# A two-layer attention encoder: part of the output product is enlarged in block A's stage, and its sum with x goes from VectorE to ScalarE and GpSimd

## Chip, cores, metric

The kernel runs on one core of one Trainium2 chip. The metric is the device time of one execution in microseconds (us), the median of three. TensorE (PE) multiplies, VectorE (DVE), ScalarE (ACT) and GpSimd (POOL) work element by element, and SyncE's queue (SP) issues the DMA transfers. A copy out of PSUM, the memory into which PE writes, is called an eviction.

## What is computed

The reference runs two layers over x (1024 rows by 1024 features). Cut to what matters:

```python
for l in range(2):
    h = rms_norm(x, norm_g[l]);  proj = h @ w_in[l]
    ya = dilated_attention(qa, ka, va, slopes) * silu(ag)   # block A: 4 heads
    yb = dense_attention(qb, kb, vb) * silu(bg)             # block B: 6 heads
    yc = dense_attention(qc, kc, vc) * silu(cg)             # block C: 6 heads
    y  = concatenate([ya, yb, yc])                          # 1024 features
    x  = x + y @ w_out[l]
```

Everything is fp32. Each product is done as three matmuls: both factors are split into a high part and a low part (hi and lo), and hi·hi, hi·lo and lo·hi are summed in PSUM.

## The kernel before

**Stages.** Each layer runs through the projections, six dense heads (block B), block A's stage, six dense heads (block C) and the out stage. In the profiled execution block A's stage lies at about 440 to 530 us in layer 0 and 1165 to 1255 us in layer 1.

**Order.** The heads and block A are written as small functions (`qk`, `soft`, `tv_t`, `a_s`, `a_t`, `f_mm` and so on) that `put(slot, f, priority)` enters in a table; slots are walked in order, and within a slot by priority. ACT executes in the order of this program. For PE, DVE, POOL and SP a scheduler decides the order ahead of time, and every engine then keeps to its own list: an instruction that waits holds up all that stand behind it on its engine.

**Block A's heads.** For each head `a_s` multiplies queries and keys into PSUM (L889 to L895), DVE adds a table and takes minima (L902, L905), ACT takes exponentials (L912, L914). A chain of small steps then finds the scales of three patterns: DVE L943, ACT L948, DVE L954, L955, L956, L958 and L961, PE L969 and DVE L975. GpSimd multiplies the probabilities by the scales, 8 times L984 (window patterns) and 8 times L988 (class pattern) for each head. PE transposes them (L1001, L1006, L1007), ACT and DVE split the result into hi and lo (L774, L775), and PE multiplies with the values (L1030 to L1044, first line for each form).

**The early part of the out product.** y is held as eight chunks of 128 features. Chunk k is split into `yh[k]` and `yl[k]` by `fin_split` (ACT L828, GpSimd L829) as soon as its two heads are done. Chunks 2 and 3 come from the first four heads of block B, chunk 4 from the last two. The output has eight blocks m of 128 features. For m = 2 to 7 the products with chunks 2 and 3 are done in block A's stage, in two halves of 512 columns: `f_load` fetches the weights and splits them on GpSimd (L1091, L1092) and fetches x; `f_mm` does six matmuls for a half into one PSUM bank (L1104, L1105, L1106); `f_add` adds that bank to x on DVE (L1110); a DMA stores the sum as `x_part`. One half follows the other after two slots, one m the other after five. The out stage does the rest (L1246 to L1248) and adds `x_part`.

**Buffers.** The T tag has four PSUM banks, shared by the transposes, the small products of the chain, the heads' sums (acc) and the halves of `f_mm`. The H tag has six SBUF buffers of 128x512.

Of the kernel before, what the change touches and what calls it, by code (L numbers as in the profile page):

```python
# [9 lines left out]
F32R = mybir.dt.float32r  # L10
I32 = mybir.dt.int32
AF = mybir.ActivationFunctionType
ALU = mybir.AluOpType
AX = mybir.AxisListType

P = 128
# [6 lines left out]
AH, BH, CH = 4, 6, 6  # L23
N_U = 28

EARLY_K, EARLY_M = (2, 3), range(2, 8)


@with_exitstack
def hybrid_encoder(  # L30
# [7 lines left out]
    nc = tc.nc  # L38
    V, G, A, T = nc.vector, nc.gpsimd, nc.scalar, nc.tensor
# [9 lines left out]
    def nm(s):  # L49
        uid[0] += 1  # L50
        return f"{s}_{uid[0]}"

    def U(dt=F32, shape=(P, SEQ)):
        return sp.tile(list(shape), dt, tag="U", name=nm("u"), bufs=N_U)

    def QB(dt=F32, shape=(P, 1152)):
        return sp.tile(list(shape), dt, tag="QB", name=nm("qb"), bufs=8)

    def H(dt=F32, shape=(P, 512)):
        return sp.tile(list(shape), dt, tag="H", name=nm("h"), bufs=6)  # L60

    def WR(dt=F32, shape=(P, 512)):
        return sp.tile(list(shape), dt, tag="Wr", name=nm("wr"), bufs=3)
# [13 lines left out]
    def PT():  # L77
        return pp.tile([P, 512], F32, tag="T", name=nm("T"), bufs=4)
# [4 lines left out]
    def f32(ap):  # L83
        return ap.bitcast(F32)
# [95 lines left out]
    ws = Stream()  # L180


    def x_prepare(k, x32, g_sb, xh, xl, parts=(slice(0, SEQ),)):
        hi, lo = U(F32R), U(F32R)
        for s in parts:
            A.activation(hi[:, s], x32[:, s], AF.Copy, scale=g_sb[:, k:k + 1])
            V.scalar_tensor_tensor(lo[:, s], x32[:, s], g_sb[:, k:k + 1], f32(hi[:, s]), ALU.mult, ALU.subtract)
        xh.append(hi)
        xl.append(lo)
# [28 lines left out]
    x_scr = dp.tile([SEQ, SEQ], F32, name="x_scr")  # L218
# [37 lines left out]
    MV = 2  # L256
# [10 lines left out]
    def layer(l, xh, xl, ss, g, bg_x):  # L267
# [7 lines left out]
        x_part = dp.tile([SEQ, SEQ], F32, name=nm("x_part"))  # L275
# [6 lines left out]
        for k in range(8):  # L282
            if bg_x is not None:
                bg_x(k)
            wh, wl = ws.next(3)
# [9 lines left out]
            for m, half in order:  # L295
                w = slice(m * P, m * P + P)
                o = bk[m][half]
                s = slice(half * 512, half * 512 + 512)
# [90 lines left out]
        for k in range(8):  # L389
            w = ws.next(3)  # L390
# [37 lines left out]
        for c in range(NCH):  # L428
            s = slice(c * P, (c + 1) * P)
            pq = PS()  # L430
            for half in range(2):
                o = pq[:, half * 512:half * 512 + 288]
                w = slice(half * 288, half * 288 + 288)
# [6 lines left out]
        for c in range(NCH):  # L440
            s = slice(c * P, (c + 1) * P)
# [641 lines left out]
        Fw, Fx, Fp = {}, {}, {}  # L1083

        def f_load(m):
            n = len(EARLY_K) * P
            raw = WR()[:, :n]
            both = H(F32R)
            hi, lo = both[:, :n], both[:, n:2 * n]
            nc.sync.dma_start(raw.rearrange("p (k c) -> p k c", c=P), w_out[l, m, :, EARLY_K[0]:EARLY_K[-1] + 1, :])  # L1090
            G.tensor_scalar(hi, raw, 1.0, 1.0, ALU.mult, ALU.mult)  # L1091
            G.tensor_tensor(lo, raw, f32(hi), ALU.subtract)  # L1092
            Fw[m] = (hi, lo)
            t = Fx[m] = U()
            nc.sync.dma_start(t, (x_t if l == 0 else x_scr)[m * P:(m + 1) * P, :])

        def f_mm(m, half):
            ps = Fp[m, half] = PT()
            hi, lo = Fw[m]
            s = slice(half * 512, half * 512 + 512)  # L1100
            n = len(EARLY_K)
            for i, k in enumerate(EARLY_K):
                w = slice(i * P, i * P + P)
                T.matmul(ps, hi[:, w], yh[k][:, s], start=(i == 0), stop=False)  # L1104
                T.matmul(ps, hi[:, w], yl[k][:, s], start=False, stop=False)  # L1105
                T.matmul(ps, lo[:, w], yh[k][:, s], start=False, stop=(i == n - 1))  # L1106

        def f_add(m, half):
            t = Fx[m][:, half * 512:half * 512 + 512]
            V.tensor_tensor(t, Fp.pop((m, half)), t, ALU.add)  # L1110
            if half:
                nc.sync.dma_start(x_part[m * P:(m + 1) * P, :], Fx.pop(m))


        base_a = 16 * BH
# [10 lines left out]
        def put(s, f, pri=5):  # L1126
            at_slot.setdefault(s, []).append((pri, len(at_slot.get(s, [])), f))


        for i, hd in enumerate(heads):  # L1130
            for c in range(NCH):
                s = start[hd] + 2 * c - LAG_D
# [4 lines left out]
        def a_slot(k):  # L1137
            return base_a + AS0 + AD * k // 2

        for h in range(AH):  # L1140
            for m in range(4):
                s = a_slot(4 * h + m)
# [3 lines left out]
            s = a_slot(4 * h + 3) + 1  # L1146
# [9 lines left out]
        for i, hd in enumerate(heads):  # L1156
            for half in range(2):
                for j in range(8):
                    s = start[hd] + 8 * half + j
                    put(s, lambda hd=hd, half=half, j=j: tv_t(hd, half, j), 1)  # L1160
                    put(s + DV, lambda hd=hd, half=half, j=j: tv_v(hd, half, j), 9)
                s = start[hd] + 8 * half + 8 + DV
# [6 lines left out]
        for h in range(AH):  # L1169
            for i in range(8):  # L1170
                s = base_a + AT0 + 8 * h + i
# [4 lines left out]
                    put(base_a + AT0 + 8 * h + FA[0] + half, lambda h=h, half=half: fin_gate(h // 2, half), 6)  # L1176
                    put(base_a + AT0 + 8 * h + FA[1] + half, lambda h=h, half=half: fin_split(h // 2, half), 6)
        F0, FN, FP, FL = -10, 5, 6.5, 8
        for m in EARLY_M:
            s = base_a + F0 + FN * (m - EARLY_M[0])  # L1180
            put(s - FL, lambda m=m: f_load(m), 9)
            for half in range(2):
                put(s + 2 * half, lambda m=m, half=half: f_mm(m, half), FP)
                put(s + 2 * half + 1, lambda m=m, half=half: f_add(m, half), 6)

        turns = (-23, -22, -19, -17)
        for i, hd in enumerate(heads):
            kind, h = hd
            s = start[hd]
# [10 lines left out]
        for h in range(AH):  # L1200
            s = a_slot(4 * h)
# [34 lines left out]
        nss = QB()[:, :SEQ] if l + 1 < DEPTH else None  # L1236
        ng = load_gains(l + 1) if l + 1 < DEPTH else None

        def out_part(ps, w2, ks, halves=(0, 1)):
            for k in ks:  # L1240
                wh, wl = w2[k // 4]
                w = slice((k % 4) * P, (k % 4) * P + P)
                for half in halves:
                    s = slice(half * 512, half * 512 + 512)
                    o = ps[half] if isinstance(ps, list) else ps[:, s]
                    T.matmul(o, wh[:, w], yh[k][:, s], start=(k == 0), stop=False)  # L1246
                    T.matmul(o, wh[:, w], yl[k][:, s], start=False, stop=False)  # L1247
                    T.matmul(o, wl[:, w], yh[k][:, s], start=False, stop=(k == 7))  # L1248

        def out_half(m, ps, half):  # L1250
            s = slice(half * 512, half * 512 + 512)
            xr = H()
            nc.sync.dma_start(xr, (x_part if m in EARLY_M else x_scr)[m * P:(m + 1) * P, s])
            V.tensor_tensor(xr, ps, xr, ALU.add)
            nc.sync.dma_start(out_t[m * P:(m + 1) * P, s], xr)

        def out_end(m, ps):
            xr = QB()[:, :SEQ]
            src = x_part if m in EARLY_M else x_t if l == 0 else x_scr
            nc.sync.dma_start(xr, src[m * P:(m + 1) * P, :])  # L1260
            V.tensor_tensor(xr, ps, xr, ALU.add)
            if l + 1 < DEPTH:
                nc.sync.dma_start(x_scr[m * P:(m + 1) * P, :], xr)
                x_prepare(m, xr, ng["x"], nxh, nxl)
                x_square(m, xr, nss)
            else:
                nc.sync.dma_start(out_t[m * P:(m + 1) * P, :], xr)
# [5 lines left out]
        first = {}  # L1273

        def out_first(m, k):
            if k == 0:
                first[m] = (PS(), [ws.next(), ws.next()])
            out_part(*first[m], [k])

        todo = [(m, k) for m in range(2) for k in range(7) if (m not in EARLY_M or k not in EARLY_K)]  # L1280
        for i, (m, k) in enumerate(todo):
            put(min(end, end - OF + i * ON // 2), lambda m=m, k=k: out_first(m, k), OP)
        slots(end + 1)
        for m in range(2):
            out_part(*first[m], [7])
            out_end(m, first[m][0])
        for m in range(2, 8):
            if m == 7 and l + 1 == DEPTH:
                w2 = [ws.next(), ws.next()]
                both = [PT(), PT()]  # L1290
                for half in range(2):
                    out_part(both, w2, [k for k in range(8) if m not in EARLY_M or k not in EARLY_K], (half,))
                    out_half(m, both[half], half)
                break
            ps = PS()
            out_part(ps, [ws.next(), ws.next()], [k for k in range(8) if m not in EARLY_M or k not in EARLY_K])
            out_end(m, ps)
        return nxh, nxl, nss, ng

# [1 line left out]
    for l in range(DEPTH):  # L1301
        for k in range(8):
            ws.add(w_lat[l, k * P:(k + 1) * P, :], (P, 384))
        for k in range(8):
            ws.add(w_v[l, k * P:(k + 1) * P, :], (P, 416))
        for k in range(8):
            ws.add(w_c[l, k * P:(k + 1) * P, :], (P, 512))
        for k in range(8):
            ws.add(w_a[l, k * P:(k + 1) * P, :], (P, 512))
        for m in range(8):  # L1310
            for kh in range(2):
                ws.add(w_g[l, m, :, 4 * kh:4 * kh + 4, :], (P, 4, P))
        ws.hold()
        for m in range(8):
            n = EARLY_K[0] if m in EARLY_M and EARLY_K[-1] == 3 else 4
            ws.add(w_out[l, m, :, 0:n, :], (P, n, P), True, V if m >= MV else None)
            ws.add(w_out[l, m, :, 4:8, :], (P, 4, P), True, V if m >= MV else None)


    warm = PT()  # L1320
# [126 lines left out]
```

## Time and profile before

| | |
|---|---|
| median of three | 1462.73 us (1462.49 to 1464.2) |
| profiled execution, its own time | 1465.32 us |
| its span, first to last instruction | 1463.4 us |
| mean granted TensorE clock | 0.999 |
| PE busy | 1445.4 us, 99% |
| DVE busy | 1094.0 us, 75% |
| ACT busy | 899.0 us, 61% |
| POOL busy | 570.8 us, 39% |

The profiled execution took 2.6 us more than the median, and 1.9 us of it lie outside the span. A share is an average over the whole span; the engines' loads in block A's stage differ from it and stand in a group of their own below. A matmul of 512 columns is listed with a duration of 0.39 us, but matmuls overlap, and what one costs PE is the distance from its start to the next one's.

### The profile page before, as it was taken

The numbers are of one execution on the slowest core, as the hardware profiler recorded it, in microseconds if no ns is written. First come the engines' busy times: TensorE is split into PE (matmuls) and PEld (weight loads), VectorE is DVE, ScalarE is ACT, GpSimd is POOL, SyncE is SP. The second block draws the span as 40 slices with busy tenths as digits, with TensorE's granted clock in tenths as the row PEclk, the third lists the DMA queues.
The fourth block names the chain that finished last, engine by engine and source line by source line (L and its number), as shares of the span: only waits on it lengthen the run. The fifth ranks groups of instructions, "written<-read, shape, count | busy, mean of one in ns | idle before, by whom it ended". The sixth has DMA issues, their size and how long they took to land.

```text
span 1463.4 us, 23131 instructions
## 1 busy us (share of the span) xinstructions
PE 1445.4 (99%) x7912; PEld 1228.4 (84%) x7912; DVE 1094.0 (75%) x1997; ACT 899.0 (61%) x1678; POOL 570.8 (39%) x516
## 2 busy tenths in 40 slices
PE   9999999999999999999999999999999999999999
PEld 7998888888888888888889988888888888888887
DVE  6749767488888889994726597574888788899932
ACT  6563234488888779893425723353888886899720
POOL 5304441135455465550322054211454555655400
PEclk9999999999999999999999999999999999999999
DMA  6272126710286831112522611465103688121142
GB/s 214 78 252 62 52 98 209 211 44 30 50 200 200 243 90 44 44 34 93 192 81 82 246 37 51 158 199 162 58 30 75 167 250 226 30 60 28 58 160 101
DMA packets 118134, 171.81 MB, mean 117 GB/s; under 512 B 11520, under 2 KB 72320, under 8 KB 118016
## 3 DMA queue, kind: packets, MB, share of 16 engines
q1 hardware_dynamic: 118016, 170.32, 38.2%
q8 instruction: 63, 1.03, 0.3%
q14 instruction: 55, 0.45, 0.1%
HBM read 109.47 MB, written 60.82 MB: 116 GB/s over the span
## 4 chain that ended last, share of the span: by engine, by line
PE 90%; DVE 5%; ACT 2%; DMA 1%; issue 1%; POOL 0%; SPq 0%; ACTq 0%; DVEq 0%; POOLq 0%
PE S L752 15%; PE T L781 11%; PE acc L794 6%; PE acc L793 6%; PE T L661 4%; PE T L659 4%; PE T L660 4%; PE S L1248 3%; PE S L1246 3%; PE S L1247 3%; PE S L215 2%; PE S L214 2%; PE S L213 2%; PE T L697 1%; PE T L215 1%
## 5 line engine op out<-in xcount | busy, mean ns | idle before, releaser
L775 DVE TENSOR_TENSOR wl<-T,wh 128x512 fp32r<-128x512 f32 x440 | 296.7, 685 | 69.9 <-ACT wh L774 67.7
L774 ACT ACTIVATE wh<-T 128x512 fp32r<-128x512 f32 x440 | 261.0, 596 | 112.7 <-PE T L781 78.1
L768 POOL TENSOR_SCALAR u<-u,rec 128x1024 f32<-128x1024 f32 x192 | 216.0, 1125 | 279.8 <-DVE rec L767 164.1
L752 PE MATMUL S<-u,u 96*128 96x512 f32 (+1 forms) x960 | 269.2, 410 | 0.4
L754 DVE TENSOR_REDUCE nmax<-S 128x1 f32<-128x1024 f32 x192 | 233.5, 1216 | 24.0 <-PE S L752 23.4
L781 PEld LDWEIGHTS T<-ident,u 128*128 128x128 f32 x1536 | 190.8, 140 | 49.0 <-DVE wl L775 0.4
L781 PE MATMUL T<-ident,u 128*128 128x128 f32 x1536 | 230.0, 272 | 0.0
L761 ACT ACTIVATE u<-S,nmax 128x1024 f32<-128x1024 f32 x192 | 213.2, 1110 | 0.3
L142 POOL TENSOR_TENSOR wl<-wr,wh 128x512 fp32r<-128x512 f32 (+2 forms) x48 | 75.1, 1567 | 321.6 <-ACT wh L138 310.7
L752 PEld LDWEIGHTS S<-u,u 96*128 96x128 f32 (+1 forms) x960 | 167.1, 189 | 27.8 <-ACT u L761 1.2
L138 ACT ACTIVATE wh<-wr 128x512 fp32r<-128x512 f32 (+2 forms) x96 | 56.9, 596 | 157.6 <-PE S L214 97.3
L659 PE MATMUL T<-u,wh 128*128 128x512 f32 x256 | 102.1, 399 | 0.0
L661 PE MATMUL T<-u,wl 128*128 128x512 f32 x256 | 100.1, 391 | 0.0
L660 PE MATMUL T<-u,wh 128*128 128x512 f32 x256 | 99.9, 390 | 0.0
L793 PE MATMUL acc<-wh,u 128*128 128x512 f32 x192 | 84.5, 440 | 0.0
L793 PE MATMUL acc<-wh,qb 128*128 128x512 f32 x192 | 82.8, 431 | 0.0
L794 PE MATMUL acc<-wl,u 128*128 128x512 f32 x192 | 76.1, 396 | 2.5 <-DVE wl L775 2.5
L1246 PE MATMUL S<-u,qb 128*128 128x512 f32 x196 | 78.0, 398 | 0.0
L1248 PE MATMUL S<-u,qb 128*128 128x512 f32 x196 | 77.1, 394 | 0.0
L1247 PE MATMUL S<-u,qb 128*128 128x512 f32 x196 | 76.8, 392 | 0.0
L794 PE MATMUL acc<-wl,qb 128*128 128x512 f32 x192 | 76.1, 396 | 0.1
L142 DVE TENSOR_TENSOR wl<-wr,wh 128x512 fp32r<-128x512 f32 (+2 forms) x48 | 41.3, 861 | 44.5 <-ACT wh L138 44.4
(294 smaller groups left out, 3330.3 us busy)
## 6 DMA issues: line engine op xcount, KB each, us to landing
u<-qk_c SPq DMA_DIRECT2D x40, 256.0 KB, 4.8
wr<-in_w_g_dram SPq DMA_DIRECT2D x32, 256.0 KB, 2.6
gates<-h SPq DMA_DIRECT2D x32, 256.0 KB, 2.5
qk_c<-u SPq DMA_DIRECT2D x16, 512.0 KB, 4.1
u<-gates SPq DMA_DIRECT2D x16, 512.0 KB, 4.5
qb<-qk_a SPq DMA_DIRECT2D x32, 256.0 KB, 6.0
vb<-u SPq DMA_DIRECT2D x16, 384.0 KB, 3.3
u<-vb SPq DMA_DIRECT2D x12, 512.0 KB, 4.6
```

The lines of the kernel that those rows point to most:

```text
L659: T.matmul(ps[half], wh[:, w], xh[k][:, s], start=(k == 0), stop=False)
L660: T.matmul(ps[half], wh[:, w], xl[k][:, s], start=False, stop=False)
L661: T.matmul(ps[half], wl[:, w], xh[k][:, s], start=False, stop=(k == 7))
L752: T.matmul(ps[:, w], q[:, s], k[:, w], start=(i == 0), stop=(i == len(terms) - 1))
L754: V.tensor_reduce(nmax, ps, op=ALU.max, axis=AX.X, negate=True)
L761: A.activation(p, ps, AF.Exp, bias=nmax, accum_out=den)
L768: G.tensor_scalar(p, p, rec, 1.0, ALU.mult, ALU.mult)
L774: A.activation(ph, ps, AF.Copy)
L775: V.tensor_tensor(pl, ps, f32(ph), ALU.subtract)
L781: T.transpose(ps[:, i * P:(i + 1) * P], Pt[hd, 4 * half + i][0][:, j * P:(j + 1) * P], ident)
L793: T.matmul(acc, w, ph, start=(j == 0), stop=False)
L794: T.matmul(acc, w, pl, start=False, stop=(j == 7))
```

## The change

A table `EARLY` says for each m which chunks are done early. For m = 2, 3 and 4 these stay 2 and 3; for m = 5, 6 and 7 chunk 4 comes in. A half of those m has nine matmuls in place of six, and the out stage three fewer. `f_load` then splits 128x384 in place of 128x256 and takes two H buffers, since hi and lo no longer fit in one. For all twelve halves of a layer `f_add` takes one more H buffer: ACT copies the PSUM bank into it, and GpSimd adds it to x. The rest (`late`, `out_part`) keeps the indices of the remaining weights in step.

```diff
-EARLY_K, EARLY_M = (2, 3), range(2, 8)
+EARLY = {2: (2, 3), 3: (2, 3), 4: (2, 3), 5: (2, 3, 4), 6: (2, 3, 4), 7: (2, 3, 4)}
+
+def late(m):
+    e = EARLY.get(m, ())
+    n = e[0] if e else 4
+    return tuple(range(n)), tuple(k for k in range(n, 8) if k not in e)
...
         def f_load(m):
-            n = len(EARLY_K) * P
+            ks = EARLY[m]
+            n = len(ks) * P
             raw = WR()[:, :n]
-            both = H(F32R)
-            hi, lo = both[:, :n], both[:, n:2 * n]
-            nc.sync.dma_start(raw.rearrange("p (k c) -> p k c", c=P), w_out[l, m, :, EARLY_K[0]:EARLY_K[-1] + 1, :])
+            if 2 * n <= 512:
+                both = H(F32R)
+                hi, lo = both[:, :n], both[:, n:2 * n]
+            else:
+                hi, lo = H(F32R)[:, :n], H(F32R)[:, :n]
+            nc.sync.dma_start(raw.rearrange("p (k c) -> p k c", c=P), w_out[l, m, :, ks[0]:ks[-1] + 1, :])
             G.tensor_scalar(hi, raw, 1.0, 1.0, ALU.mult, ALU.mult)
             G.tensor_tensor(lo, raw, f32(hi), ALU.subtract)
...
-            n = len(EARLY_K)
-            for i, k in enumerate(EARLY_K):
+            n = len(EARLY[m])
+            for i, k in enumerate(EARLY[m]):
                 w = slice(i * P, i * P + P)
...
         def f_add(m, half):
             t = Fx[m][:, half * 512:half * 512 + 512]
-            V.tensor_tensor(t, Fp.pop((m, half)), t, ALU.add)
+            c = H()
+            A.activation(c, Fp.pop((m, half)), AF.Copy)
+            G.tensor_tensor(t, c, t, ALU.add)
             if half:
                 nc.sync.dma_start(x_part[m * P:(m + 1) * P, :], Fx.pop(m))
```

What this does to the engines' lists is shown at three places of layer 0. Line numbers after the change are higher by 8 up to L1088 (L984 is L992 and L988 is L996); `f_mm` is L1116 to L1118, the copy L1123, the add L1124 and `f_load`'s split L1103 and L1104.

PE, second half of m = 5. u_3371 and u_3372 are `yh` and `yl` of chunk 2, u_4066 and u_4067 of chunk 3, and the rows behind them are head 0's window transposes and head 1's scale product. Before:

```order
L1104 MATMUL T_5133<-u_3371,h_4858 128x512
L1105 MATMUL T_5133<-u_3372,h_4858 128x512
L1106 MATMUL T_5133<-u_3371,h_4858 128x512
L1104 MATMUL T_5133<-u_4066,h_4858 128x512
L1105 MATMUL T_5133<-u_4067,h_4858 128x512
L1106 MATMUL T_5133<-u_4066,h_4858 128x512
L1006 MATMUL T_5163<-ident,u_4467 128x128
L1007 MATMUL T_5163<-ident,u_4467 128x128
```

And now:

```order
L1117 MATMUL T_5152<-u_4067,h_4864 128x512
L1118 MATMUL T_5152<-u_4066,h_4865 128x512
L1116 MATMUL T_5152<-u_4834,h_4864 128x512
L1117 MATMUL T_5152<-u_4835,h_4864 128x512
L1118 MATMUL T_5152<-u_4834,h_4865 128x512
L1014 MATMUL T_5186<-ident,u_4467 128x128
L1015 MATMUL T_5186<-ident,u_4467 128x128
L1014 MATMUL T_5186<-ident,u_4467 128x128
L1015 MATMUL T_5186<-ident,u_4540 128x128
L977 MATMUL T_5197<-z_5105,order_2206 128x32
```

Three matmuls with chunk 4 (u_4834 and u_4835) came in ahead of the transposes.

ACT around the first half of m = 5. Before, an exponential's second piece, two of L774's splits and the eviction of a class sum (L1077):

```order
L774 ACTIVATE wh_5095<-T_5090 128x512
L912 ACTIVATE u_5068,st_4935<-u_5068,st_4935 128x256
L914 ACTIVATE u_5068,st_4935<-u_5068,st_4935 128x256
L774 ACTIVATE wh_5117<-T_5112 128x512
L1077 ACTIVATE u_5129<-acc_5101 64x512
```

And now:

```order
L782 ACTIVATE wh_5112<-T_5107 128x512
L920 ACTIVATE u_5085,st_4946<-u_5085,st_4946 128x256
L922 ACTIVATE u_5085,st_4946<-u_5085,st_4946 128x256
L1123 ACTIVATE h_5128<-T_5072 128x512
L782 ACTIVATE wh_5136<-T_5131 128x512
L1085 ACTIVATE u_5148<-acc_5118 64x512
```

The copy of the half came in between the exponentials and the next split.

POOL before head 0's scaling. Before, the split of chunk 4's first half (L829), and then the sixteen scalings of head 0, of which the first four rows are shown:

```order
L846 TENSOR_TENSOR u_4297<-h_4723,h_4721 64x512
L814 TENSOR_TENSOR u_4297<-u_4297,u_4295 128x512
L829 TENSOR_TENSOR u_4829<-u_4297,u_4828 128x512
L984 TENSOR_SCALAR u_4467<-u_4467,sc_4869 128x192
L984 TENSOR_SCALAR u_4467<-u_4467,sc_4869 128x256
L984 TENSOR_SCALAR u_4540<-u_4540,sc_4869 128x256 x2
L984 TENSOR_SCALAR u_4595<-u_4595,sc_4869 128x256 x2
```

And now:

```order
L854 TENSOR_TENSOR u_4297<-h_4727,h_4725 64x512
L822 TENSOR_TENSOR u_4297<-u_4297,u_4295 128x512
L1103 TENSOR_SCALAR h_4864<-wr_4863 128x384
L1104 TENSOR_TENSOR h_4865<-wr_4863,h_4864 128x384
L1124 TENSOR_TENSOR u_4562<-h_4802,u_4562 128x512
L837 TENSOR_TENSOR u_4835<-u_4297,u_4834 128x512
L1124 TENSOR_TENSOR u_4562<-h_4891,u_4562 128x512
L992 TENSOR_SCALAR u_4467<-u_4467,sc_4876 128x192
L992 TENSOR_SCALAR u_4467<-u_4467,sc_4876 128x256
```

Two adds of m = 3 (u_4562) came in, one on each side of chunk 4's split, and the second stands right ahead of head 0's scalings.

## Rows read from the trace of the kernel before

**Rows 1.** The page: busy time of the engines; the chain that ended last.

```profile
PE 1445.4 (99%) x7912; PEld 1228.4 (84%) x7912; DVE 1094.0 (75%) x1997; ACT 899.0 (61%) x1678; POOL 570.8 (39%) x516
...
PE 90%; DVE 5%; ACT 2%; DMA 1%; issue 1%; POOL 0%; SPq 0%; ACTq 0%; DVEq 0%; POOLq 0%
```

**Rows 2.** PE's waits, whole run: waiter, releaser, total us, times, longest.

```profile
PE T L969 <- DVE z L961: 3.8, 4, 1.7
PE acc L794 <- DVE wl L775: 2.5, 4, 0.8
PE T L929 <- DVE wl L1018: 1.3, 4, 0.5
PE S L889 <- DVE st L905: 1.1, 2, 0.5
```

**Rows 3.** Busy time by stretch: both layers' block A stage, last the out stage.

```profile
core 0: us, PE busy (x) PEld busy (x) DVE busy (x) ACT busy (x) POOL busy (x), PEclk, DMA share, GB/s
440.00:470.00 30.00, 29.19 (x183) 24.92 (x182) 25.35 (x98) 26.00 (x85) 12.72 (x20) 1.00 0.66 183
470.00:510.00 40.00, 38.36 (x284) 33.77 (x283) 32.93 (x118) 28.99 (x93) 22.86 (x45) 1.00 0.89 252
510.00:520.00 10.00, 8.29 (x55) 7.62 (x56) 8.60 (x15) 3.80 (x7) 7.55 (x13) 0.85 0.92 286
1170.00:1200.00 30.00, 29.67 (x188) 25.66 (x187) 25.24 (x97) 24.53 (x81) 15.05 (x25) 1.00 0.81 222
1200.00:1240.00 40.00, 38.06 (x283) 33.20 (x281) 34.31 (x115) 28.40 (x87) 21.60 (x39) 1.00 0.86 251
1240.00:1250.00 10.00, 8.58 (x69) 7.87 (x69) 8.88 (x19) 6.50 (x13) 8.89 (x19) 1.00 0.29 72
1390.00:1450.00 60.00, 60.00 (x271) 49.06 (x270) 18.23 (x25) 9.59 (x18) 0.00 (x0) 1.00 0.40 143
```

**Rows 4.** PE in order of time: second half of m = 5, and what follows.

```profile
478.94 0.39 PE L1104 MATMUL T<-u,h 128*128 128x512 f32 x1
...
480.11 0.39 PE L1106 MATMUL T<-u,h 128*128 128x512 f32 x1
480.61 0.33 PE L1006 MATMUL T<-ident,u 128*128 128x128 f32 x1
```

**Rows 5.** Groups by form: the DVE add; the ACT eviction of 128x512.

```profile
L1110 DVE TENSOR_TENSOR u<-T,u x24: 676/690/693, 448.0 to 1230.0; 128x512 f32<-128x512 f32 x24
...
L774 ACT ACTIVATE wh<-T x46: 573/597/602, 430.3 to 533.7; 128x512 fp32r<-128x512 f32 x46
```

**Rows 6.** POOL's groups by form in 435 to 535 us.

```profile
L846 POOL TENSOR_TENSOR u<-h,h 64x512 f32<-64x512 f32 x3 | 3.9, 1289 | 7.4 <-ACT h L845 7.3
L1092 POOL TENSOR_TENSOR h<-wr,h 128x256 fp32r<-128x256 f32 x5 | 3.7, 734 | 0.1
...
L814 POOL TENSOR_TENSOR u<-u,u 128x512 f32<-128x512 f32 x2 | 2.6, 1284 | 0.1
L1091 POOL TENSOR_SCALAR h<-wr 128x256 fp32r<-128x256 f32 x5 | 2.0, 408 | 0.1
```

**Rows 7.** Head 3's chain: POOL and DVE in order of time, then PE.

```profile
511.33 3.05 POOL L812 TENSOR_TENSOR u<-u,u 128x512 f32<-128x512 f32 x2 [4.68 <-issue]
...
511.83 1.09 DVE L954 TENSOR_TENSOR t<-st,e 128x16 f32<-128x16 f32 x1
512.96 1.46 DVE L955 TENSOR_TENSOR rc<-t 128x8 f32<-128x8 f32 x1
...
515.77 0.38 PE L969 MATMUL T<-z,order 128*128 128x32 f32 x2 [1.71 <-DVE z L961]
...
518.38 0.42 PE L1032 MATMUL acc<-wh,qb 128*64 128x256 f32 x1
```

**Rows 8.** The same step of head 1's chain, on DVE, POOL idle beside it.

```profile
479.59 0.17 DVE L955 TENSOR_TENSOR rc<-t 128x8 f32<-128x8 f32 x1
```

**Rows 9.** The halves of m = 3 and m = 5 on DVE; ACT at those places.

```profile
456.75 0.69 DVE L1110 TENSOR_TENSOR u<-T,u 128x512 f32<-128x512 f32 x1 [0.42 <-PE T L1106]
...
474.90 0.68 DVE L1110 TENSOR_TENSOR u<-T,u 128x512 f32<-128x512 f32 x1
...
460.12 0.58 ACT L774 ACTIVATE wh<-T 128x512 fp32r<-128x512 f32 x1
...
480.50 0.58 ACT L774 ACTIVATE wh<-T 128x512 fp32r<-128x512 f32 x1
```

**Rows 10.** POOL around head 0's scalings and chunk 4's split; PE's class transposes.

```profile
465.34 3.55 POOL L984 TENSOR_SCALAR u<-u,sc 128x192 f32<-128x192 f32 x8 [1.25 <-DVE sc L958]
468.86 3.20 POOL L988 TENSOR_SCALAR u<-u,s2c 128x256 f32<-128x256 f32 x7
...
476.66 0.72 POOL L1092 TENSOR_TENSOR h<-wr,h 128x256 fp32r<-128x256 f32 x1
478.23 1.30 POOL L829 TENSOR_TENSOR u<-u,u 128x512 fp32r<-128x512 f32 x1 [0.85 <-ACT u L828]
...
471.33 0.60 PE L1001 MATMUL T<-ident,u 128*128 128x128 f32 x4
```

More of the change, by code (lines that the diff above doesn't have):

```diff
@@ L1178, in layer @@
         F0, FN, FP, FL = -10, 5, 6.5, 8
-        for m in EARLY_M:
-            s = base_a + F0 + FN * (m - EARLY_M[0])
+        for i, m in enumerate(EARLY):
+            s = base_a + F0 + FN * i
             put(s - FL, lambda m=m: f_load(m), 9)
@@ L1237, in layer, with out_part @@
         ng = load_gains(l + 1) if l + 1 < DEPTH else None
-        def out_part(ps, w2, ks, halves=(0, 1)):
+        def out_part(m, ps, w2, ks, halves=(0, 1)):
             for k in ks:
-                wh, wl = w2[k // 4]
-                w = slice((k % 4) * P, (k % 4) * P + P)
+                piece = 0 if k in late(m)[0] else 1
+                wh, wl = w2[piece]
+                i = late(m)[piece].index(k)
+                w = slice(i * P, i * P + P)
                 for half in halves:
@@ L1252, in out_half @@
             xr = H()
-            nc.sync.dma_start(xr, (x_part if m in EARLY_M else x_scr)[m * P:(m + 1) * P, s])
+            nc.sync.dma_start(xr, (x_part if m in EARLY else x_scr)[m * P:(m + 1) * P, s])
             V.tensor_tensor(xr, ps, xr, ALU.add)
@@ L1258, in out_end @@
             xr = QB()[:, :SEQ]
-            src = x_part if m in EARLY_M else x_t if l == 0 else x_scr
+            src = x_part if m in EARLY else x_t if l == 0 else x_scr
             nc.sync.dma_start(xr, src[m * P:(m + 1) * P, :])
@@ L1277, in out_first @@
                 first[m] = (PS(), [ws.next(), ws.next()])
-            out_part(*first[m], [k])
-        todo = [(m, k) for m in range(2) for k in range(7) if (m not in EARLY_M or k not in EARLY_K)]
+            out_part(m, *first[m], [k])
+        todo = [(m, k) for m in range(2) for k in range(7) if k in sum(late(m), ())]
         for i, (m, k) in enumerate(todo):
@@ L1284, in layer @@
         for m in range(2):
-            out_part(*first[m], [7])
+            out_part(m, *first[m], [7])
             out_end(m, first[m][0])
@@ L1291, in layer @@
                 for half in range(2):
-                    out_part(both, w2, [k for k in range(8) if m not in EARLY_M or k not in EARLY_K], (half,))
+                    out_part(m, both, w2, sum(late(m), ()), (half,))
                     out_half(m, both[half], half)
@@ L1295, in layer @@
             ps = PS()
-            out_part(ps, [ws.next(), ws.next()], [k for k in range(8) if m not in EARLY_M or k not in EARLY_K])
+            out_part(m, ps, [ws.next(), ws.next()], sum(late(m), ()))
             out_end(m, ps)
@@ L1314, in hybrid_encoder @@
         for m in range(8):
-            n = EARLY_K[0] if m in EARLY_M and EARLY_K[-1] == 3 else 4
-            ws.add(w_out[l, m, :, 0:n, :], (P, n, P), True, V if m >= MV else None)
-            ws.add(w_out[l, m, :, 4:8, :], (P, 4, P), True, V if m >= MV else None)
+            for ks in late(m):
+                ws.add(w_out[l, m, :, ks[0]:ks[-1] + 1, :], (P, len(ks), P), True, V if m >= MV else None)
     warm = PT()
```

## The prediction

> **What bounds the kernel now.** I read the page first. PE is busy 99% of the span and carries 90% of the chain that ended last [rows 1]. So a change pays only where PE stands still, or where it gives PE less to do. I then read what PE waits for [rows 2]. The longest waits belong to block A's stage (L969, L929, L889), all for DVE; L794's belong to the dense heads. Third came the loads by stretch [rows 3]. In 440 to 470 and 470 to 510 us of layer 0, PE is idle 0.81 and 1.64 us, and in the same places of layer 1 0.33 and 1.94 us: 4.7 us in all. The next ten microseconds of each layer (510 to 520, 1240 to 1250) lose 1.7 and 1.4 us more, by a wait of their own, below. In 440 to 510 DVE is busy 58.3 of 70 us, ACT 55.0 and POOL 35.6. The out stage has no idle PE at all: 60.00 of 60 us. So the stage that gives work away is bound by PE alone, and the stage that takes it is PE at 96 to 99% with small stops that other engines end.
>
> **Moved matmuls.** In each layer three m's get three more matmuls in each of two halves, 18; in both layers 36. Their price is the distance between starts. From L1104 at 478.94 to the sixth of that half at 480.11 there are five distances, 0.234 us each [rows 4]. So 36 x 0.234 = 8.4 us leave the out stage, which has no idle time to lose them in, and 8.4 us enter block A's stage, 4.2 us a layer or 0.70 us a half. If PE were busy throughout there too, the net would be zero. What is won is the idle time that they fill. The enlarged halves (m = 5 to 7) lie in about 470 to 510 us, where PE idles 1.64 us, and 1.94 us in layer 1: 3.6 us [rows 3]. The bounds are 0 (the stops are set by chains that are pushed back by as much) and 3.6. I take 3.6, since 4.2 us a layer enter in six pieces, more than twice the idle time, and each piece needs only weights and finished chunks.
>
> **The add leaves DVE.** L1110 runs 24 times at 0.69 us [rows 5], 8.3 us a layer. DVE's load in 440 to 510 falls from 58.3 to 50.0 us of 70 [rows 3]. PE's waits in this stage are for DVE [rows 2], so in the earlier stretch, where no half is enlarged, part of the 0.81 + 0.33 = 1.1 us goes too. Bounds 0 and 1.1; I take 0.6, about half, because those stops follow ACT's splits as well as DVE's. The later stretch's relief is already counted above and not again.
>
> **The copy on ACT.** The nearest row is an eviction of the same shape, L774, 0.597 us [rows 5]. Twelve a layer are 7.2 us: ACT goes from 55.0 to 62.2 us of 70. The tight place is 440 to 470 of layer 0: ACT is at 26.0 of 30, and four or five copies (m = 2, 3 and the start of m = 4) make it about 28.7; in layer 1 24.5 becomes 27.2. There a late eviction holds PE. I charge one copy's length in each layer, 0.6 x 2 = 1.2 us. Bounds: 0 if the copies fall into ACT's gaps, and 4 x 0.6 x 2 = 4.8 if every copy of m = 2 and 3 delays PE's next transposes by its length.
>
> **The add on GpSimd.** The nearest rows are the tensor-by-tensor L814 and L846, 1.28 and 1.29 us [rows 6]. Twelve a layer are 15.4 us. The split of `f_load` grows by half for three m's: 3 x 0.5 x (0.73 + 0.41) = 1.7 us [rows 6]. POOL's 35.6 us of 70 become about 52, so there is room. What hides it is that nobody in this stage waits for `x_part`: the out stage reads it tens of microseconds later. What is queued behind it does matter. The second add of m = 3 stands right ahead of head 0's scalings, which began at 465.34 us with POOL idle for 1.25 us before them [rows 10]. If the copy comes in time the add goes into that gap; if it comes late, all sixteen scalings move by up to 1.3 us, and the class transposes that began at 471.33, while the last scalings still ran, move too. Between 0 and 1.3 us a layer; I take 0, nearest to the gap's row. At m = 5 the new matmuls need chunk 4's split, L829 at 478.23 to 479.53, with idle POOL ahead of it from 477.38 [rows 10]. Behind one add (1.28) and the longer `f_load` (0.57) it would end at about 480.5. The six older matmuls of that half run until about 480.35 [rows 4]. A stop of 0 to 0.5 us a layer; I take 0, since the first two figures nearly meet.
>
> At this point a rule speaks against the change. The Trainium skill, "GPSIMD Engine Reference", Specifications, says that GpSimd shares its SBUF interfaces with VectorE and contends with DVE instructions that have two SBUF inputs; by that page's opening the Vector engine is also about twice as fast at elementwise arithmetic. The trace agrees, below. By the rule the sum would carry the third rival's price; by the rows I keep that as a rival.
>
> What the rows show: while POOL ran two L812 from 511.33 to 514.38, DVE's L954 took 1.09 us and L955 1.46 us, on tiles of 16 and 8 columns [rows 7]. The same L955 took 0.17 us in head 1, POOL idle [rows 8]. PE then stood 1.71 us at L969. L812 is not touched by the change and no add lies behind m = 7's, so these 1.7 us stay in both layers. In layer 0 PE's granted clock fell behind that wait (0.85 over 510 to 520, against 1.00 in layer 1 [rows 3]; L1032 runs 0.42 us [rows 7]): part of the stretch at 1.2 GHz in place of 2.4. I leave it as it is. The price of a change in it is about 15% of 10 us, 1.5 us, in either direction: gone in layer 0, or new in layer 1.
>
> **Sum.** Against the profiled execution's 1465.32 us: -8.4 + 8.4 (moved) - 3.6 (filled) - 0.6 (relief) + 1.2 (ACT) = -3.0, so 1462.3. That execution lay 2.6 us above the median, so the median should come to **1459.7 us**.
>
> **Rival 1, slower: the halves hold their PSUM bank too long.** ACT works in program order, so the copy stands behind exponentials that wait for DVE. At the first half of m = 5, DVE was done at 475.58 (474.90 + 0.68). The copy now stands just ahead of the split that ACT began at 480.50 [rows 9]; at the pace of before, the bank comes free at about 481.1, 5.5 us later. At m = 3 it is 457.44 against about 460.7. A half's bank is one of four, which transposes and head sums share. If PE then stops for 0.3 us a half on the mean over 24 halves, that is 7.2 us, and -3.0 + 7.2 = +4.2: 1466.9. It is slower from about 0.25 us a half. For it: 5.5 us is longer than a transpose's bank is used. Against it: with DVE relieved the exponentials come earlier, and in 440 to 520 and 1170 to 1250 ACT had 42 us without work before, for 14 us of copies [rows 3].
>
> **Rival 2, no change: the fill is eaten.** The stops in 470 to 510 end with chains through DVE, ACT and POOL. The enlarged halves stand ahead of PE's own steps of these chains (at m = 5 ahead of the window transposes and of the scale product, as the rows of PE show), so 0.7 us of work goes in, and the chain ends up to 0.7 us later. With the fill at 1.0 instead of 3.6, relief and ACT as above: -0.4, 1462.3. That the change does nothing because PE bounds both stages alike ends in the same place.
>
> **Rival 3, slower: the adds block DVE.** Of each head's chain three DVE instructions (L943, L954, L955) read two small SBUF tiles. Twelve adds of 1.28 us fill 15.4 of about 70 us in a layer, so a fifth to a quarter of these steps would meet one. A meeting costs 1.46 - 0.17 = 1.3 us at most [rows 7, 8]. If in each layer two heads are hit in two of their steps and PE waits for all of it, 2 x 2 x 2 x 1.1 = 8.8 us, and -3.0 + 8.8 = +5.8: 1468.5. It decides from about three such hits a layer that reach PE. Against it: only one chain of four reaches PE as a long wait today [rows 2].
>
> **Numbers.** The forecast has 0.43, rival 2 has 0.32, rival 1 0.16 and rival 3 0.09. A difference below 0.2%, 2.9 us, can hardly be told from none here, so faster means below 1459.8, slower above 1465.7. The forecast lies at the edge of that: faster 0.43, same 0.33, slower 0.24. Its own range is 1456 to 1462. The lower end of the whole takes all idle time of both stretches (4.7), no cost on ACT, the clock's 1.5 and a third of the long waits (1.1 of 3.4): 1462.7 - 7.3 = 1455.4; I say 1455. The upper end is between the two slower rivals, 1467.5.
>
> **What would show it.** Right: the moved matmuls at 0.23 us in block A's stage; PE idle below 1 us in the enlarged stretch of each layer; the out stage 4.2 us shorter a layer; DVE near 50 of 70 us; L1124 at 1.28 us. Wrong: waits of PE for ACT's L1123 or for the banks that it frees (rival 1), for GpSimd's L992, L996 or L837 (POOL's queue), L951, L962 or L963 of DVE above 0.7 us beside L1124 (rival 3), a new stretch at 1.2 GHz, or more than 4.2 us a layer gained by block A's stage in length.

## The result and the profile after

The changed kernel takes 1479.57 us (median of four runs, 1478.91 to 1480.23) against 1463.47 us of the kernel before in the same comparison. The ratio is 1.0111, with a 95% interval of 1.0099 to 1.0123: 16 us slower, outside the range of 1455 to 1467.5. The sign is that of rivals 1 and 3. The first link of the chain, a wait for an H buffer, is one that none of them names.

The page of the changed kernel, the parts that answer to [rows 1]:

```profile
PE 1446.6 (98%) x7912; PEld 1230.8 (83%) x7912; DVE 1077.9 (73%) x1973; ACT 912.1 (62%) x1702; POOL 604.9 (41%) x540
...
PE 90%; DVE 3%; ACT 2%; POOL 2%; issue 1%; DMA 1%; SPq 0%; ACTq 0%; DVEq 0%; POOLq 0%
```

PE's busy time hardly grew. DVE lost 16 us, ACT gained 13 and POOL 34, as the change says. What is new is POOL's 2% of the chain that ended last, where it had none. The waits of PE over the whole run, answering to [rows 2]:

```profile
PE T L1116 <- ACT h L1123: 11.5, 2, 5.8
PE T L977 <- DVE z L969: 5.5, 4, 1.7
...
PE T L1009 <- ACT h L1123: 1.5, 2, 0.8
PE T L1116 <- ACT h L853: 1.3, 2, 0.7
...
PE T L937 <- DVE wl L1026: 1.0, 2, 0.5
```

Two waits, one a layer and 5.8 us long, make up most of the loss, 11.5 of 16 us: a first matmul of `f_mm` waits for the copy on ACT. Here is that place in layer 0, on PE, ACT and POOL in order of time:

```profile
472.29 0.61 PE L1009 MATMUL T<-ident,u 128*128 128x128 f32 x4
478.65 0.80 PE L1116 MATMUL T<-u,h 128*128 128x512 f32 x1 [5.75 <-ACT h L1123]
479.25 0.63 PE L1117 MATMUL T<-u,h 128*128 128x512 f32 x1
...
480.95 0.63 PE L1118 MATMUL T<-u,h 128*128 128x512 f32 x1
...
471.97 0.49 ACT L922 ACTIVATE u<-u,st 128x256 f32<-128x256 f32 x1
...
478.00 0.60 ACT L1123 ACTIVATE h<-T 128x512 f32<-128x512 f32 x1 [5.45 <-POOL u L854]
...
470.16 1.85 POOL L996 TENSOR_SCALAR u<-u,s2c 128x256 f32<-128x256 f32 x4
471.98 1.27 POOL L1124 TENSOR_TENSOR u<-h,u 128x512 f32<-128x512 f32 x1
473.22 1.85 POOL L996 TENSOR_SCALAR u<-u,s2c 128x256 f32<-128x256 f32 x4
475.04 0.52 POOL L1103 TENSOR_SCALAR h<-wr 128x384 fp32r<-128x384 f32 x1
475.64 0.99 POOL L1104 TENSOR_TENSOR h<-wr,h 128x384 fp32r<-128x384 f32 x1
476.71 1.26 POOL L854 TENSOR_TENSOR u<-h,h 64x512 f32<-64x512 f32 x1
```

Read it from the bottom. L854 adds two halves of a block B head's sum, which ACT had put in two H buffers. It stands in GpSimd's list behind head 0's scalings, an add and the longer weight split, and ends at 477.97. The copy of m = 4's second half needs an H buffer and gets the one that L854 gives back: ACT stands for 5.45 us. That copy empties the PSUM bank into which PE puts the first half of m = 5: PE stands for 5.75 us, and with it all that is behind it. Nothing on PE, ACT or PSUM is too slow here; a ring of six SBUF buffers is full, and its release stands in the most crowded part of GpSimd's list. Before, the same head sum (L846) ran three microseconds earlier, and ACT asked for no buffer for a copy:

```profile
473.67 1.28 POOL L846 TENSOR_TENSOR u<-h,h 64x512 f32<-64x512 f32 x1
```

After the wait PE runs at the lower level of its clock (1.2 GHz) for a while. The starts from 479.25 to 480.95 are four distances of 0.425 us, against 0.234 before [rows 4]. In layer 1 the whole half runs so:

```profile
1210.54 0.79 PE L1116 MATMUL T<-u,h 128*128 128x512 f32 x1 [5.76 <-ACT h L1123]
...
1214.12 0.63 PE L1118 MATMUL T<-u,h 128*128 128x512 f32 x1
```

From the first to the ninth start are 3.58 us here and 3.29 us in layer 0 (478.65 to 481.94). Eight distances of 0.234 would be 1.87, so the lower clock cost about 3.1 us in both layers together, an estimate from these starts. With the 11.5 us of waits that is nearly the whole loss. The loads by stretch, answering to [rows 3], show the clock and the idle time:

```profile
440.00:470.00 30.00, 27.80 (x173) 23.83 (x173) 21.78 (x90) 26.29 (x83) 17.19 (x21) 1.00 0.58 164
470.00:510.00 40.00, 33.27 (x225) 29.51 (x225) 21.70 (x91) 26.68 (x84) 26.36 (x41) 0.96 0.71 211
1200.00:1240.00 40.00, 33.27 (x219) 29.48 (x218) 20.67 (x89) 25.96 (x81) 27.26 (x42) 0.91 0.68 204
...
479.00:483.00 4.00, 4.00 (x16) 3.30 (x16) 2.06 (x9) 2.90 (x11) 1.56 (x2) 0.68 0.40 135
```

PE's idle time grew from 0.81 to 2.20 us in 440 to 470, and from 1.64 to 6.73 us in 470 to 510. In the second stretch the load of PE, ACT and DVE fell (DVE's also because its adds are gone), and POOL's rose.

### The profile page after: what moved, and what is told of

Same layout as the page of the kernel before. It is cut to its first block, busy times and chain, and to the rows that moved or that the text cites. A ratio compares the mean times of both kernels' runs of the same rounds, so it can differ in the third digit from the quotient of the medians.

```text
span 1477.1 us, 23134 instructions
## 1 busy us (share of the span) xinstructions
PE 1446.6 (98%) x7912; PEld 1230.8 (83%) x7912; DVE 1077.9 (73%) x1973; ACT 912.1 (62%) x1702; POOL 604.9 (41%) x540
## 3 DMA queue, kind: packets, MB, share of 16 engines
q8 instruction: 62, 1.02, 0.3%
## 4 chain that ended last, share of the span: by engine, by line
PE 90%; DVE 3%; ACT 2%; POOL 2%; issue 1%; DMA 1%; SPq 0%; ACTq 0%; DVEq 0%; POOLq 0%
PE S L760 15%; PE T L789 11%; PE acc L802 6%; PE acc L801 6%; PE T L667 4%; PE T L668 4%; PE T L669 4%; PE S L1264 3%; PE S L1262 3%; PE S L1263 3%; PE S L221 2%; PE S L223 2%; PE S L222 2%; PE T L705 1%; PE T L221 1%
## 5 line engine op out<-in xcount | busy, mean ns | idle before, releaser
L783 DVE TENSOR_TENSOR wl<-T,wh 128x512 fp32r<-128x512 f32 x440 | 297.1, 686 | 91.9 <-ACT wh L782 90.1
L802 PE MATMUL acc<-wl,u 128*128 128x512 f32 x192 | 76.1, 396 | 2.5 <-DVE wl L783 2.5
L802 PE MATMUL acc<-wl,qb 128*128 128x512 f32 x192 | 76.1, 397 | 0.1
L1262 PE MATMUL S<-u,qb 128*128 128x512 f32 x186 | 74.1, 398 | 0.0
L1264 PE MATMUL S<-u,qb 128*128 128x512 f32 x186 | 73.2, 394 | 0.0
L1263 PE MATMUL S<-u,qb 128*128 128x512 f32 x186 | 72.9, 392 | 0.0
```

Of the source, the lines that this page charges most:

```text
L783: V.tensor_tensor(pl, ps, f32(ph), ALU.subtract)
L802: T.matmul(acc, w, pl, start=False, stop=(j == 7))
```

## Experiments

Theory A: the H ring, by the chain above. Rivals: ACT comes late to copies and PSUM banks are held (B, rival 1 of the prediction); GpSimd's adds block DVE's two-input steps (C, its rival 3). Ratios are against the kernel before on the same chip, with 95% intervals.

### More H buffers

```diff
-        return sp.tile(list(shape), dt, tag="H", name=nm("h"), bufs=6)
+        return sp.tile(list(shape), dt, tag="H", name=nm("h"), bufs=8)
...
-            den = SM(1, "den", 6)
+            den = SM(1, "den", 5)
```

> The changed kernel with eight H buffers in place of six (one small scratch tag has five buffers in place of six, to make room). Theory A: the loss of about 16 us comes from the H tag. The copy of block m = 4's second half finds no free H buffer until GpSimd's L854 has read one, ACT stands 5.45 us, and PE behind it 5.8 us a layer, with a stretch at 1.2 GHz after it. With two more buffers both waits go: 11.5 us of waits and some 2 to 3 us of half clock less, so 1463 to 1467 us. Theory B: the halves hold PSUM banks too long because ACT comes late to every copy, whatever the buffers: no more than 3 us less, 1476 to 1480. Theory C: the adds on GpSimd block DVE's two-input steps: PE's waits for L969 and L937 stay at 6.5 us against 5.1 before, and the time is 1472 or more.

Measured: 1469.54 us, 1.0037 (1.0024 to 1.0050). The same with `bufs=7` and six `den`:

> The changed kernel with seven H buffers. Theory A: one more buffer gives the copy a buffer that is released earlier (an older f_load weight or an earlier copy), so most of the 5.8 us wait goes: 1463 to 1472 us, between the changed kernel and the one with eight. Theory B: 1476 to 1480. Theory C: 1472 or more.

Measured: 1471.49 us, 1.0044 (1.0027 to 1.0061). One more buffer takes back 0.67% of the 1.11%, two 0.74%, about 11 us. PE's waits with eight:

```profile
PE T L977 <- DVE z L969: 5.5, 4, 1.7
PE T L1116 <- DVE wl L783: 3.4, 2, 1.9
...
PE T L1116 <- ACT h L1123: 2.0, 2, 1.0
PE T L1009 <- ACT h L1123: 1.6, 2, 0.8
PE T L1116 <- ACT h L853: 1.3, 2, 0.7
```

The 5.8 us waits are gone, so A holds for the greater part. But the time stays 5 us above before, outside A's 1463 to 1467. L977's waits stay at 5.5 us, as C said, but the time is below C's 1472. Two copies still wait for a buffer, 1.4 us in all, now for an add (L1124).

### The buffer's holder, by name

With six buffers, the sums of the last two block B heads go to DVE, which takes one half straight from PSUM. The other half is still copied into an H buffer, but DVE gives that one back, and L854 is gone there:

```diff
-        ADD_DVE = [('c', h) for h in range(CH)]
+        ADD_DVE = [('c', h) for h in range(CH)] + [('b', 4), ('b', 5)]
```

> The changed kernel with its six H buffers (1479.6 us); only the last two block B heads' sums (L854) are added by DVE straight from PSUM, so that GpSimd's L854 no longer holds two H buffers there. Theory A, with the culprit by name: the copy of m = 4's second half waits for the buffers that L854 gives back behind nine scalings and a weight split, so without it ACT's 5.45 us wait goes or falls to about 1 us (the next buffer to come free is that of the add ahead): 1467 to 1473 us, like seven or eight buffers. If it stays above 1477, it wasn't L854 but the length of the ring as such.

Measured: 1468.57 us, 1.0033 (1.0022 to 1.0045), within the expectation and as good as eight buffers. The copy then waits for nothing but PE, 2.0 us in the whole run:

```profile
ACT h L1123 <- PE T L1118: 2.0, 2, 1.0
```

So the long wait hangs on the buffers behind L854: with them out of GpSimd's list six are enough. (The sum also asks the ring for one buffer fewer, which this run does not separate.) And the 5 us that are left are not the ring's, since no copy waits for a buffer here.

### The two parts of the change alone

Larger shares, the add left on DVE, no copy:

```diff
-            c = H()
-            A.activation(c, Fp.pop((m, half)), AF.Copy)
-            G.tensor_tensor(t, c, t, ALU.add)
+            V.tensor_tensor(t, Fp.pop((m, half)), t, ALU.add)
```

> Only the larger shares: chunk 4 for m = 5 to 7, but the add stays on DVE, from PSUM, and there is no copy; six H buffers. Theory A: without the copy ACT never asks for an H buffer for it, so no long wait; the moved 8.4 us fill idle time of PE: 1458 to 1463. Theory B: the same. If the larger shares themselves are the cause (two H buffers for the weights), the head's sums in tv_end wait for buffers: 1468 or more.

Measured: 1462.09 us, 0.9987 (0.9977 to 0.9996). The busy time of PE, DVE, ACT and POOL in the stretches of the enlarged halves:

```profile
470.00:510.00 40.00, 39.06 (x279) 34.66 (x277) 31.30 (x109) 27.54 (x90) 23.24 (x44) 1.00 0.90 256
1200.00:1240.00 40.00, 38.81 (x278) 33.94 (x277) 31.45 (x102) 26.98 (x82) 19.52 (x36) 1.00 0.84 238
```

PE idles 0.94 and 1.19 us there, against 1.64 and 1.94 before [rows 3]: 1.45 us filled out of 3.6, in stretches with the same bounds. L889's wait of [rows 2] is gone, and L937's (L929 before) has grown from 1.3 us:

```profile
PE T L937 <- DVE wl L1026: 2.2, 4, 0.6
```

Copy and GpSimd add alone, chunks 2 and 3 for all m, six buffers:

```diff
-EARLY = {2: (2, 3), 3: (2, 3), 4: (2, 3), 5: (2, 3, 4), 6: (2, 3, 4), 7: (2, 3, 4)}
+EARLY = {m: (2, 3) for m in range(2, 8)}
```

> Only the copy on ACT and the add on GpSimd, with chunks 2 and 3 for all m, so weights take one H buffer each; six H buffers. Theory A: the ring of six is asked for fewer buffers, the copy finds one earlier: 1461 to 1468. Theory B: late copies hold banks here as well: 1470 or more. Theory C: as many adds as in the changed kernel, so most of its loss: 1472 or more.

Measured: 1473.48 us, 1.0061 (1.0045 to 1.0077), above A's range. PE's waits:

```profile
PE T L977 <- DVE z L969: 5.5, 4, 1.7
PE T L1116 <- DVE wl L783: 3.8, 2, 1.9
...
PE T L1116 <- ACT h L1123: 2.1, 2, 1.1
```

Weights in one H buffer leave the ring room: the 5.8 us wait isn't there, and two copies wait 1.5 us in all for a buffer. So it takes both parts together to fill the ring, and yet the copy and the add on their own cost 9 us, as B and C would both have it.

### Copy and add apart

Both with eight H buffers and larger shares, one line changed each:

```diff
-            G.tensor_tensor(t, c, t, ALU.add)
+            V.tensor_tensor(t, c, t, ALU.add)
```

> Eight H buffers, larger shares, the copy on ACT as in the change, but the sum of the copy and x on DVE instead of GpSimd. The same with GpSimd took 1469.5 us, and larger shares with one DVE add and no copy 1462.1. Theory A2: what is left of the loss comes from ACT's copy, which stands late in ACT's order and holds a PSUM bank (L1116 and L1009 wait 3.6 us for L1123, L1116 1.3 for L853): 1467 to 1470 us. Theory C: it comes from the adds on GpSimd, which stop DVE's two-input steps (L969 took 1.03 us beside an add and PE stood 1.1 us for it) and stand ahead of other work of GpSimd: 1462 to 1465.

Measured: 1471.43 us, 1.0042 (1.0028 to 1.0056), above A2's range, with runs from 1467.3 to 1472.5. The profiled run is the one of 1467.3, with a mean granted clock of 1.000; the three above 1471 have 0.998. So the waits below are not all of this median.

```diff
-            A.activation(c, Fp.pop((m, half)), AF.Copy)
+            V.tensor_copy(c, Fp.pop((m, half)))
```

> Eight H buffers, larger shares, the copy out of PSUM on DVE instead of ACT, and the add on GpSimd as in the change. Theory A2: DVE frees the bank about when it did before, so the waits for L1123 go: 1462 to 1465 us. Theory C: GpSimd's adds are all still there, 24 of 1.28 us: 1467 or more. If both have a share it lies between, and the two parts add up to about 7 us.

Measured: 1466.93 us, 1.0024 (1.0014 to 1.0034), between the two ranges. With the copy on ACT and the add on DVE, PE's waits are these:

```profile
PE T L1116 <- DVE wl L783: 3.7, 2, 1.9
PE T L977 <- DVE z L969: 3.4, 2, 1.7
PE acc L802 <- DVE wl L783: 3.3, 6, 0.8
PE T L1009 <- ACT h L1123: 1.6, 2, 0.8
PE T L1116 <- ACT h L853: 1.3, 2, 0.7
```

And with the copy on DVE and the add on GpSimd, these:

```profile
PE T L977 <- DVE z L969: 6.1, 4, 1.6
PE T L1009 <- POOL u L996: 3.2, 4, 1.4
...
PE T L937 <- DVE wl L1026: 2.0, 4, 0.5
...
PE T L1117 <- POOL u L837: 0.8, 2, 0.4
```

The signatures differ; what they share is two waits of about 1.7 us at L977, which the kernel before has too [rows 2]. ACT's copy makes PE wait for splits and copies that ACT reaches late. GpSimd's add makes it wait for head 0's scalings (L996), for chunk 4's split (L837) and, by DVE, for L969. Each alone costs 5 to 8 us over the version without copy, both together 7: they hide each other in part, and the two prices don't add up to 7, as the expectation had it.

### Controls with eight buffers

> Larger shares, one DVE add and no copy, and eight H buffers. If the H tag holds nothing up where no copy asks for it, as in theory A, it equals the same kernel with six: 1460 to 1463.5 us. If the two buffers for the weights of m = 5 to 7 cost something with six, it is faster: below 1460.

Measured: 1462.08 us, 0.9989 (0.9980 to 0.9999).

> The kernel before with eight H buffers: the control for the two more buffers and the smaller scratch tag. All theories: no change, 1462 to 1466 us, within 0.2% of the kernel before. If it is faster or slower by more, the runs with eight buffers are to be read against it.

Measured: 1462.05 us, 0.9989 (0.9979 to 0.9998). Two more buffers alone bring about 0.1%, and with them the larger shares bring nothing more. The clock has a part in both: nine of the ten runs of the kernel before with eight buffers have a mean granted clock of 1.000, one of ten with the larger shares on top, and eight of 25 of the kernel before. Those eight have a median of 1462.58 us. Why the clock falls less often in one version, no run shows. Costs with eight buffers are therefore taken from 0.9989 upwards.

### The copy's place in ACT's order

```diff
-                put(s + 2 * half + 1, lambda m=m, half=half: f_add(m, half), 6)
+                put(s + 2 * half + 1, lambda m=m, half=half: f_add(m, half), 0)
```

> The changed kernel with eight H buffers (1469.5 us) and one number more: each copy and add is entered first in its slot instead of behind the exponentials, so that ACT comes to a copy a split earlier at m = 3 and m = 5. Theory A2: the copy's late place in ACT's order holds PSUM banks; L1116's waits for L1123 and L783 (5.4 us) and L1009's for L1123 (1.6) shrink by half or more: 1465 to 1467 us. Rival: ACT has simply 7.2 us more to do a layer, and a copy moved ahead makes the next split late by as much: 1468.5 to 1471.

Measured: 1467.24 us, 1.0026 (1.0017 to 1.0035). PE's waits:

```profile
PE T L977 <- DVE z L969: 4.0, 4, 1.7
PE acc L802 <- DVE wl L783: 3.7, 6, 0.8
PE T L1116 <- ACT h L1123: 2.6, 4, 1.0
PE T L937 <- DVE wl L1026: 2.3, 4, 0.7
```

L1116's waits for L783 (3.4 us) and L1009's for L1123 (1.6) are gone, and those of L1116 for L1123 are 2.6 in place of 2.0. Other waits have grown: L802's from 2.5 to 3.7, L937's from 1.0 to 2.3, L897's from 0.4 to 1.3. So A2 and the rival each have a part, and the time lies between their ranges. It falls by 0.11%, and the two intervals overlap. Then the same, with copy and GpSimd add for m = 5 to 7 only (the DVE add of m = 2 to 4 keeps its old place in the slot):

```diff
+            if m < 5:
+                V.tensor_tensor(t, Fp.pop((m, half)), t, ALU.add)
+            else:
+                c = H()
+                A.activation(c, Fp.pop((m, half)), AF.Copy)
+                G.tensor_tensor(t, c, t, ALU.add)
```

> Eight H buffers, larger shares, and the copy and add entered first in their slot, but only for m = 5 to 7; m = 2 to 4 keep the one DVE add. With the copy for all m this took 1467.2 us, with one DVE add for all 1462.1. Theory D: what is left of the loss comes from the stretch of m = 2 to 4, where ACT is already at 26 of 30 us and the add of m = 3 lies on head 0's chain: then this version loses nearly nothing, 1461 to 1464 us. Rival: every copy and add costs about the same, wherever it stands, so half of the 5 us is left: 1464 to 1466.

Measured: 1463.43 us, 1.0001 (0.9991 to 1.0011). Of the 0.37% between 0.9989 and 1.0026, 0.25% go with the six halves a layer of m = 2 to 4, and 0.12% stay. The time lies in theory D's range, and by it the early stretch carries two thirds. But the interval takes in the 1.0008 that half of the loss would leave, so the rival isn't excluded.

### DVE and GpSimd beside each other

Larger shares, the add on DVE, six buffers, and the gate product on DVE too:

```diff
-                G.tensor_tensor(gv, yv, gv, ALU.mult)
+                V.tensor_tensor(gv, yv, gv, ALU.mult)
```

> A version that might beat both: larger shares and DVE add (1462.1 us), and the strided gate product of block A's heads (L820, two at 1.55 us, beside which DVE's L962 and L963 take 1.1 and 1.46 us and PE stands 1.7 us a layer) on DVE instead of GpSimd. If GpSimd's two-input work blocks DVE's small steps (theory C), both long waits of PE for L969, 3.4 us, go, and with them the stretches at 1.2 GHz: 1457 to 1460 us, less two DVE products of some 0.7 to 1.5 us if they come ahead of the same chain. If those steps are slow for another reason, 1461 to 1464.

Measured: 1463.96 us, 1.0002 (0.9992 to 1.0011): no gain over the 0.9987 of the same kernel with the product on GpSimd. On DVE in layer 0:

```profile
513.72 0.18 DVE L962 TENSOR_TENSOR t<-st,e 128x16 f32<-128x16 f32 x1
513.81 1.09 DVE L820 TENSOR_TENSOR u<-u,u 128x512 f32<-128x512 f32 x1
514.81 0.17 DVE L963 TENSOR_TENSOR rc<-t 128x8 f32<-128x8 f32 x1
...
516.23 1.03 DVE L820 TENSOR_TENSOR u<-u,u 128x512 f32<-128x512 f32 x1
517.17 0.19 DVE L969 TENSOR_TENSOR z<-sc,order 128x32 f32<-128x32 f32 x1
```

Without GpSimd's product beside them the small steps take 0.18 and 0.17 us instead of 1.09 and 1.46 [rows 7], so their length was GpSimd's doing, although the time lies in the range that was given to another reason. But the products now stand in DVE's own list ahead of L963 and L969, and PE still waits 1.3 us.

## Why the prediction was wrong

**The step that failed** is "What hides it is that nobody in this stage waits for `x_part`", together with a sum that has no term for H buffers. The text priced engines, PSUM banks and queues, and the diff's `c = H()` and the second buffer of `f_load` nowhere. A consumer there is: whoever next needs an H buffer. It turned up as a wait of ACT for GpSimd that before did not exist. By h8 and b5_dve it is worth 0.74 to 0.78%, 11 us of the 16.

**POOL has room** was right on average (43.6 of 70 us in 440 to 510, where about 52 were reckoned) and wrong at the place. Between 470 and 478 us GpSimd's list had no gap, and the two adds and the longer split pushed L854 three microseconds back.

**The copy on ACT** was mis-sized: 1.2 us taken, bounds 0 and 4.8. With the add on DVE it costs 0.53% of 1464, 7.8 us over 0.9989. DVE does one add a half there as before, but is busy 1099.0 us against the 1092.9 of the larger shares alone; neither this part nor that of the lower clock is separated by a run. The mechanism was the stated one, ACT late for PE, and the place only in part: in layer 0 of that run PE's waits of 440 to 470 us grew by 0.9 us (L1116 for L853, L802 for L783), and 2.6 us came behind 470 (L1116 for L783, L1009 for L1123).

**The add on GpSimd** was taken at 0, with bounds of 1.3 us a layer for head 0's scalings and 0.5 for chunk 4. In the changed kernel the scalings began at 466.62, 1.28 us later than before, the whole of the first bound. With the copy on DVE PE's waits are 1.6 a layer (L996) and 0.4 (L837). The bound of chunk 4 held, the other was a little short, and the value taken was wrong in both.

**Rival 3** named the right mechanism and the wrong instruction. In the changed kernel DVE and POOL stand so at head 0:

```profile
465.66 1.02 DVE L969 TENSOR_TENSOR z<-sc,order 128x32 f32<-128x32 f32 x1
...
465.37 1.26 POOL L1124 TENSOR_TENSOR u<-h,u 128x512 f32<-128x512 f32 x1 [1.50 <-ACT h L1123]
...
466.83 0.38 PE L977 MATMUL T<-z,order 128*128 128x32 f32 x2 [1.09 <-DVE z L969]
```

L969, a product with two SBUF inputs that the rival's list leaves out, ends with the add of m = 3's second half, and PE waits for L969: 1.1 us a layer. One hit a layer reached PE, where the rival's price needed four. The Trainium skill, "GPSIMD Engine Reference", Specifications, says that the two engines contend for an SBUF interface when DVE has two SBUF inputs; the trace agrees, 1.02 us against 0.19 in head 1.

**Rival 1** named the place where PE was seen to wait (a bank behind L1123) and a price, 1466.9, near what is left without the ring: 1469.5. The bank in question was that of m = 4's second half, not those of m = 3 and 5 that the rival followed, and the copy was late for want of a buffer, not behind exponentials.

**The moved matmuls.** Their price in the out stage was right: in layer 1 the last matmul of the heads (L794, now L802) and the last of the out stage start 52.4 us apart, from 1420.7 to 1473.1, where they were 56.5 apart. That is 4.1 us less, and 4.2 were reckoned. The fill was taken at its bound, 3.6 us. Measured, 1.45 us of idle time went and the time fell by 0.13%, 1.9 us, with six buffers; with eight, by nothing. The stops that remain end with chains through DVE: L937's wait for L1026 is 2.2 us instead of 1.3. That was rival 2's argument. The relief of DVE was seen in no run by itself.

**The clock** was left as it is, with 1.5 us in either direction. It cost something new behind the long waits of both layers, about 3.1 us by the estimate above.

The larger shares with a DVE add and the kernel before with eight buffers are the fastest versions run, each about 0.1% below the kernel before; the difference is smaller than the 0.2% that the text sets as its bound, so neither is claimed as a gain.

## What to carry to other kernels

An edit that takes one more buffer from a shared ring can add a wait for whoever releases the next one: look up which engine that is, and what stands ahead of the release in its list, before pricing the engines. Moving an instruction off a busy engine pays only if a wait of the bound engine ends with that instruction or behind it in the list. Here PE waited for DVE's adds for 0.3 us in the whole run before, and their replacement touched two in-order lists instead of one:

```profile
PE T L1001 <- DVE u L1110: 0.3, 2, 0.2
```

Room on average says nothing of a place: take the list of that engine in the ten microseconds where the new work lands.

## What was not expected of the hardware

How long GpSimd's tensor-by-tensor add holds a small DVE step shows as its remaining length: L969 took 1.02 us beside an add that ended at 466.63, 0.97 us after L969 began, and 0.19 in head 1 at 486.58, with POOL idle when it began. Beside scalings the rows are mixed: L951 took 0.42 us at 473.33 beside L996, against 0.17 at 460.80, and L969 took 0.19 beside L992 with the gate product on DVE. In the stretch of 479 to 483 us, behind a stand of 5.75 us, the granted clock was 0.68 on average, with matmuls at 0.425 us from start to start; in 1200 to 1240, around the same stand in layer 1, it was 0.91.
